# A replanned instruction order and moved query tiles in a one-core decoder trunk

## The chip, the cores and the metric

The kernel runs on one core of one Trainium2 chip. The time is the device time of one execution in microseconds (us). Five engines work side by side, each through its own instructions in program order: PE (matrix products, with PEld for its weight loads), DVE (vector work), ACT (activations and copies), POOL and SP, which here issues nearly all transfers.

## The reference

Two layers over x of 256 positions by 1024 channels. Each layer normalises x, multiplies it by one combined input matrix (1024 x 9808), runs three causal mixers of 8 heads with 64 channels each, gates each mixer's output, projects it to 1024 channels, merges the three by sigmoid gates, multiplies by an output matrix and adds the residual. A final normalisation follows.

```python
h = rms_norm(x, gain)
proj = jnp.einsum('bsd,de->bse', h, w_in)
(qa, ka, va, ga, qb, kb_, vb_, gb, qc, kc, vc, gc,
 q_idx, k_idx, w_idx, f_logit, merge_logit) = jnp.split(proj, SPLIT_POINTS, axis=-1)
oa = moba_attention(rope(qa), rope(ka), va) * jax.nn.silu(ga)              # with 256 positions: plain causal attention
ob = dsa_attention(rope(qb), rope(kb_), vb_, qi, ki, wi) * jax.nn.silu(gb) # the 64 best keys of each query by an index score
oc = forgetting_attention(qc, kc, vc, log_f) * jax.nn.silu(gc)             # a forget bias is added to the scores
y = jnp.einsum('nbsw,nwd->bsnd', jnp.stack([oa, ob, oc]), w_branch)
merged = jnp.sum(jax.nn.sigmoid(merge_logit) * y, axis=2)
return x + jnp.einsum('bsd,de->bse', merged, w_out)
```

## The kernel before

Everything is float32 in and out. To keep that precision PE multiplies split numbers: an operand is cut into a high part and a low remainder, and a product is high x high, low x high and high x low, three matmuls. The tiles ending in h and l (hTh and hTl, og0h and og0l, wh and wl) are such pairs.

Weights come from memory in pieces of 0.5 or 1 MB, read by SP into one of four raw tiles (line 436 for most). ACT writes the high part (wh, line 444) and DVE the remainder (wl, line 448); six tiles of each go round. PE multiplies from them at line 486 in units of 24 matmuls of 256 columns, or 12 for a branch projection, each unit into one of three proj tiles of PSUM. A proj tile comes free only when ACT or DVE has read the unit's result: line 986 (tanh of a merge gate into a mth tile, ACT), line 1017 (gate times branch projection, DVE), and others.

A mixer works on four pairs of heads. For a pair, `write_q` (line 683) makes three query tiles of 128 x 256: qh holds the high parts of both heads, and qx and qy are the tiles for the first and the second head, each with the high part of its head in one half of the partitions and a low part in the other. `scores` (line 698) runs six matmuls against the key tiles bd: the query tiles are the loaded weights, in two blocks of 128 columns, and the keys are streamed, 256 and 128 columns for the first block of queries and 512 and 256 for the second. Then come the softmax on DVE and ACT (lines 775 to 794, the last being the low part of the probabilities, "p lo"), one transfer that transposes each head's probabilities (line 803, issued by SP), the copies of the result into pt (lines 808 on ACT, 809 on DVE), and the eight matmuls of the product with the values, here called av (lines 821 to 824, two heads in turn). What follows av is the gating of the pair (lines 837 to 842, 476, 477).

The order of all instructions on every engine is fixed when the program is built. The kernel records some 3,300 operations with a key each; `Plan.run` places them one after the other by estimated costs and, among those of an engine that could start at about the same time, takes the smallest key. Two tables correct it: `SHIFT` adds a number to the key of the operation with that number, and `WAY` raises or lowers the cost of DVE for an operation that has DVE and another engine to choose from. The estimated costs themselves are not touched by the change. For wh and wl tiles a helper, `shifted`, states where the two sorts of tile begin:

```python
return [slice((a - base) % 512 // 4, (a - base) % 512 // 4 + 1024) for a, base in zip(at, (128, 0))]
```

wh tiles begin at 128 modulo 512 bytes of a partition, and wl tiles at 0. By the sizes of what stands between, all nine query tiles of before begin at 128.

Of the kernel before, what the change touches and what calls it, by code (L numbers as in the profile page):

```python
# [10 lines left out]
F32R = mybir.dt.float32r  # L11
# [5 lines left out]
S = 256  # L17
# [46 lines left out]
def constants(forget_bias):  # L64
# [24 lines left out]


SHIFT = {
# [31 lines left out]
}  # L123
WAY = {
# [6 lines left out]
}  # L131


# [173 lines left out]
def hybrid_trunk(ctx, tc, x, w_in, w_branch, w_out, final_gain, consts, out):  # L307
# [3 lines left out]
    pool = ctx.enter_context(tc.tile_pool(name="sb", bufs=1))  # L311
# [3 lines left out]
    plan = Plan()  # L315
# [32 lines left out]
    wh = [pool.tile([128, 1152], F32R, name=f"wh{i}") for i in range(R_RING)]  # L348
    fz = pool.tile([128, 6, 16], F32, name="fz")
    wl = [pool.tile([128, 1152], F32R, name=f"wl{i}") for i in range(R_RING)]  # L350
    ncs = pool.tile([128, 2, 8], F32, name="ncs")
    csum = pool.tile([128, 2, 8], F32, name="csum")
    V = [pool.tile([128, 2, 8, 128], F32R, name=f"v{i}") for i in range(2)]
    qs = [[pool.tile([128, S], F32R, name=f"q{p}{i}") for i in range(3)] for p in "hxy"]
    widx = pool.tile([128, 2, 8], F32, name="widx")
    hTh = pool.tile([128, KC, S], F32R, name="hTh")
    hTl = pool.tile([128, KC, S], F32R, name="hTl")
# [44 lines left out]
    tag("raw", R_RAW, [128, 2048])  # L402
    plan.tag("wh", wh)
    plan.tag("wl", wl)
    plan.tag("qx", qs[1])
    plan.tag("qy", qs[2])
    plan.tag("qh", qs[0])
    plan.tag("pt", pts)
    plan.tag("bd", bd)
    for nm, n, cols, dt in (("rsh", 2, S, F32), ("rr", 3, S, F32),  # L410
# [892 lines left out]
```

## Time and profile before

| | us |
|---|---|
| median of three runs | 602.27 |
| the three runs | 600.35, 602.92, 602.27 |
| the profiled execution | 601.2 |
| its span in the profile | 599.4 |
| PE busy | 587.5 |
| DVE busy | 542.3 |
| ACT busy | 463.8 |

The profile comes from one execution. A matmul's duration in it is longer than its turn on the engine, since matmuls overlap: what a matmul costs in a full row of them is the step from one start to the next. The wait table names, for each engine and line, what ended its idle time. The chain of waits goes back from the last instruction to what released it, step by step, and is a way to see which engine set the pace in each stretch. The granted clock of PE was full in every slice.

### The profile page before, as it was taken

How to read it: one execution, taken by the hardware profiler on the slowest of the kernel's cores; microseconds unless marked ns; L12 is line 12 of the kernel's file. 1: busy time of each engine (PE TensorE's matmuls, PEld its weight loads, DVE VectorE, ACT ScalarE, POOL GpSimd, SP SyncE). 2: the span in 40 equal slices, each digit the busy share in tenths (PEclk: the TensorE clock that was granted, in tenths of full speed). 3: DMA queues.
4: the chain of work that ended last, by engine and by line, in shares of the span. 5: the costliest groups of instructions: out<-in, count | busy, mean ns of one | idle time of the engine just before them, and what ended most of it. 6: DMA issues, size and time to landing. Idle time of an engine off the chain costs nothing.

```text
span 599.4 us, 12672 instructions
## 1 busy us (share of the span) xinstructions
PE 587.5 (98%) x4704; PEld 567.8 (95%) x4704; DVE 542.3 (90%) x1360; ACT 463.8 (77%) x1004; POOL 92.4 (15%) x102
## 2 busy tenths in 40 slices
PE   9999999999999999999999999999999999999995
PEld 7999999999998999999889999999999899999885
DVE  8889999989999989999686999999998999999773
ACT  5769669987997879985485874999889787999632
POOL 1042133000000225110000421320000023340000
PEclk9999999999999999999999999999999999999999
DMA  8986286597865866397648447669869486645802
GB/s 314 305 282 210 73 233 182 162 226 213 241 182 140 271 195 164 89 286 245 189 150 262 152 143 235 178 186 208 214 188 256 121 246 208 169 133 129 311 35 72
DMA packets 136510, 116.83 MB, mean 195 GB/s; under 512 B 42752, under 2 KB 127360, under 8 KB 136448
## 3 DMA queue, kind: packets, MB, share of 16 engines
q1 hardware_dynamic: 136160, 115.59, 66.4%
q8 instruction: 37, 0.61, 0.4%
q10 hardware_dynamic: 288, 0.43, 0.2%
q14 instruction: 25, 0.20, 0.1%
HBM read 103.42 MB, written 1.05 MB: 174 GB/s over the span
## 4 chain that ended last, share of the span: by engine, by line
PE 58%; DVE 22%; ACT 9%; DMA 5%; issue 4%; POOL 0%; SPq 0%; POOLq 0%; DVEq 0%; ACTq 0%
PE proj L486 47%; DVE wl L448 7%; PE proj L1173 4%; DMA t<-e 4%; ACT wh L444 2%; PE proj L1113 2%; DVE isc L970 2%; DVE e L794 1%; DVE rsh L535 1%; ACT pt L808 1%; ACT e L779 1%; DVE t L969 1%; DVE isc L949 1%; DMA raw<-in_w_out_dram 1%; DVE rr L537 1%
## 5 line engine op out<-in xcount | busy, mean ns | idle before, releaser
L486 PE MATMUL proj<-hTh,wh 128*128 128x256 f32 x1024 | 265.7, 278 | 1.5 <-ACT mth L986 1.0
L486 PE MATMUL proj<-hTl,wh 128*128 128x256 f32 x1024 | 265.0, 277 | 0.0
L448 DVE TENSOR_TENSOR wl<-raw,wh 128x1024 fp32r<-128x1024 f32 x180 | 223.3, 1249 | 15.2 <-ACT wh L444 14.0
L486 PE MATMUL proj<-hTh,wl 128*128 128x256 f32 x1024 | 227.9, 276 | 0.0
L444 ACT ACTIVATE wh<-raw 128x1024 fp32r<-128x1024 f32 x180 | 188.7, 1054 | 38.6 <-PE proj L486 26.3
L486 PEld LDWEIGHTS proj<-hTh,wh 128*128 128x128 f32 x1024 | 192.2, 188 | 2.3 <-ACT mth L986 1.2
L486 PEld LDWEIGHTS proj<-hTl,wh 128*128 128x128 f32 x1024 | 192.2, 188 | 0.0
L486 PEld LDWEIGHTS proj<-hTh,wl 128*128 128x128 f32 x1024 | 172.9, 188 | 0.0
L536 POOL TENSOR_TENSOR rsh<-rsh,cst 128x256 f32<-128x256 f32 x40 | 32.4, 812 | 351.4 <-DVE rsh L535 323.2
L538 POOL TENSOR_TENSOR rr<-rr,rsh 128x256 f32<-128x256 f32 x40 | 45.6, 1140 | 2.8
L779 ACT ACTIVATE e<-e,st 128x128 f32<-128x128 f32 (+1 forms) x96 | 42.6, 445 | 2.9 <-DVE st L775 2.4
L794 DVE SCALAR_TENSOR_TENSOR e<-e,st 128x128 f16<-128x128 f32 (+1 forms) x96 | 40.1, 424 | 1.1 <-ACT e L787 0.4
L808 ACT ACTIVATE pt<-t 128x384 fp32r<-128x384 f16 x73 | 34.3, 513 | 7.1 <-DMA t<-e 6.8
L486 PE MATMUL proj<-wh,v 128*128 128x512 f32 (+1 forms) x144 | 35.2, 366 | 0.0
L486 PE MATMUL proj<-og0l,wh 128*128 128x256 f32 x128 | 33.8, 277 | 0.0
L486 PE MATMUL proj<-og0h,wh 128*128 128x256 f32 x128 | 32.4, 278 | 1.3 <-DVE mth L1017 1.3
L787 ACT ACTIVATE e<-e,st 128x256 f16<-128x256 f32 (+1 forms) x77 | 31.6, 445 | 2.7 <-DVE st L783 2.3
L486 PEld LDWEIGHTS proj<-wh,v 128*128 128x128 f32 x144 | 25.3, 189 | 4.3
L486 PE MATMUL proj<-og0h,wl 128*128 128x256 f32 x128 | 28.6, 276 | 0.0
L486 PEld LDWEIGHTS proj<-og0h,wh 128*128 128x128 f32 x128 | 24.0, 188 | 1.6 <-DVE mth L1017 1.5
L486 PEld LDWEIGHTS proj<-og0l,wh 128*128 128x128 f32 x128 | 24.0, 188 | 0.0
L486 PEld LDWEIGHTS proj<-og0h,wl 128*128 128x128 f32 x128 | 21.7, 188 | 0.0
(227 smaller groups left out, 1071.0 us busy)
## 6 DMA issues: line engine op xcount, KB each, us to landing
raw<-in_w_in_dram SPq DMA_DIRECT2D x74, 1024.0 KB, 5.5
raw<-in_w_branch_dram SPq DMA_DIRECT2D x24, 512.0 KB, 4.2
raw<-in_w_out_dram SPq DMA_DIRECT2D x8, 1024.0 KB, 8.4
raw<-in_x_dram SPq DMA_DIRECT2D x8, 256.0 KB, 4.9
tmp<-wf SPq DMA_DIRECT2D x16, 128.0 KB, 5.5
t<-e SPq DMA_TRANSPOSE x48, 2.9
raw<-in_w_in_dram SPq DMA_DIRECT2D x2, 320.0 KB, 6.2
x<-in_x_dram SPq DMA_DIRECT2D x2, 256.0 KB, 3.8
```

The lines of the kernel that those rows point to most:

```text
L444: ACT.activation(p[0].v, sel(c.v), AF.Copy)
L448: DVE.tensor_tensor(p[1].v, sel(c.v), p[0].v.bitcast(F32), op=ALU.subtract)
L486: PE.matmul(o(), a(), b(), start=first and i == 0, stop=last and i == n - 1)
L536: gps(lambda: POOL.tensor_tensor(T(sh)[:np_], T(sh)[:np_], s[:np_], op=ALU.mult), S, [k_rope], [sh], key, "rope")
L538: gps(lambda: POOL.tensor_tensor(T(r)[:np_], T(r)[:np_], T(sh)[:np_], op=ALU.add), S, [sh], [r], key, "rope")
L779: act(lambda t=t, a=a, n=n, st=st, h=h: ACT.activation(ex(h, a, n), ex(h, a, n), AF.Exp, bias=T(st)[:, t:t + 1], scale=-1.0, accum_out=T(s ...
L787: ACT.activation(hi(a, n), ex(h, a, n), AF.Copy, scale=T(st)[:, 4 + t:5 + t])
L794: dve(lambda t=t, a=a, n=n, st=st, h=h, hi=hi, lo=lo: DVE.scalar_tensor_tensor(lo(a, n), ex(h, a, n), T(st)[:, 4 + t:5 + t], hi(a, n), op0 ...
L808: plan.op([("ACT", t_act(384, False), lambda to=to, src=src: ACT.activation(to(), src(), AF.Copy)), ("DVE", t_dve2(384), lambda to=to, src ...
L970: dve(lambda o=o, t8=t8: DVE.match_replace(o, T(t8), o, TAKEN), n, [t8], [k_isc[i]], key + r * step, "top8")
L1113: PE.matmul(T(ps[t]), h(i, t), v(w, n), start=left[t] == 23, stop=left[t] == 0)
L1173: PE.matmul(T(ps[t])[:, :w], hA[hi](a + x, t), T(p[wi])[:, ats[w > 256][wi]][:, :n * w].rearrange("p (k c) -> p k c", k=n)[:, x], start=le ...
```

## The change

Both tables are replaced, so that the order on each engine is another one while the operations, their estimated costs and the rules of the planner stay. The new numbers were found by replaying the program, outside the kernel, with a model that also counts the transfers by which the engines fetch their instructions. A few operations with a choice change their engine: in all, ACT has 73 rows of line 808 before and 72 after, DVE 23 and 24 of line 809, 28 and 27 of line 1019, 18 and 20 of line 842; POOL has 6 and 4 of line 841, 4 and 5 of line 1020.

Second, the six qx and qy tiles are allocated right behind the wl tiles, and so begin at 0 modulo 512 bytes. The three qh tiles stay behind the value tiles, at 128. All other tiles begin where they did modulo 512 bytes, and nothing else in the code changes. (The allocation gives some tiles another running number: v_78 becomes v_84.)

```diff
@@ -89,45 +89,44 @@
 SHIFT = {
-    0: -11.5, 1: -7, 3: -11.5, 4: -11, 17: 2, 28: -8, 31: -6, 47: -11, 73: 4, 80: -12, 89: -2.5, 90: -11.5, 91: 1.5,
...
+    0: -12, 1: -7.5, 3: -12, 4: -10.5, 18: -2.5, 19: -7.5, 22: -4.5, 28: -12, 31: -5.5, 38: -8, 46: -12, 47: -12,
...
 }
 WAY = {
-    17: -1500, 18: -1500, 90: -1500, 99: 1500, 489: 1500, 490: 1500, 539: 1500, 552: -1500, 553: -1500, 559: 1500,
...
+    18: 1500, 19: -1500, 46: 1500, 90: -1500, 126: -1500, 509: 1500, 534: -1500, 547: 1500, 548: -1500, 631: 1500,
...
 }
@@ -348,10 +347,11 @@
     wl = [pool.tile([128, 1152], F32R, name=f"wl{i}") for i in range(R_RING)]
+    qs = {p: [pool.tile([128, S], F32R, name=f"q{p}{i}") for i in range(3)] for p in "xy"}
     ncs = pool.tile([128, 2, 8], F32, name="ncs")
     csum = pool.tile([128, 2, 8], F32, name="csum")
     V = [pool.tile([128, 2, 8, 128], F32R, name=f"v{i}") for i in range(2)]
-    qs = [[pool.tile([128, S], F32R, name=f"q{p}{i}") for i in range(3)] for p in "hxy"]
+    qs.update({p: [pool.tile([128, S], F32R, name=f"q{p}{i}") for i in range(3)] for p in "h"})
@@ -402,9 +402,9 @@
-    plan.tag("qx", qs[1])
-    plan.tag("qy", qs[2])
-    plan.tag("qh", qs[0])
+    plan.tag("qx", qs["x"])
+    plan.tag("qy", qs["y"])
+    plan.tag("qh", qs["h"])
```

Three places of the order are spoken of below. The first is on ACT, in the first mixer of layer 0, around the first merge gate whose result goes to a mth tile (line 986). The other rows there are the copies of transposed probabilities (808), the key tiles of the third and fourth pair (852, 864), the second halves of query tiles (693, 695), the gating of the first pair (837, 476) and the high part of weights (444). Before:

```order
L808 ACTIVATE pt<-t_136 128x384 x2
L852 ACTIVATE bd1h<-rr_124 128x512
L693 ACTIVATE qx_84<-qy_87 64x256
L837 ACTIVATE ot_138<-o_159 64x256
L864 ACTIVATE bd1h<-bd1h 64x256
L693 ACTIVATE qx_83<-qy_86 64x256
L695 ACTIVATE qy_86<-qh_80 64x256
L864 ACTIVATE bd0h<-bd0h 64x256
L837 ACTIVATE ot_138<-o_159 64x256
L695 ACTIVATE qy_87<-qh_81 64x256
L864 ACTIVATE bd1h<-bd1h 64x256
L444 ACTIVATE wh_64<-raw_119 128x1024
```

and then og0h (line 476) and the two rows of line 986. After:

```order
L852 ACTIVATE bd0h<-rr_123 128x512
L864 ACTIVATE bd0h<-bd0h 64x256 x2
L808 ACTIVATE pt<-t_136 128x384
L986 ACTIVATE mth_143<-proj_152 128x256
L808 ACTIVATE pt<-t_137 128x384 x2
L444 ACTIVATE wh_68<-raw_119 128x1024
L695 ACTIVATE qy_80<-qh_87 64x256
```

The first merge gate, mth_143, has moved ahead of the second key tile, of the gating of the first pair and of one high part of weights. The second gate, mth_144, stands further back, behind the exponentials of the third pair.

The second place is on SP, at the transposes (803) of the third and fourth pair of the same mixer and the weight loads (436) between them. Before:

```order
L803 DMA_TRANSPOSE t_136<-e_128 128x6x128
L803 DMA_TRANSPOSE t_137<-e_128 128x6x128
L436 DMA raw_119<-in_w_in_dram 128x8x256
L803 DMA_TRANSPOSE t_136<-e_129 128x6x128
L436 DMA raw_117<-in_w_in_dram 128x8x256
L803 DMA_TRANSPOSE t_137<-e_129 128x6x128
```

After:

```order
L803 DMA_TRANSPOSE t_136<-e_128 128x6x128
L803 DMA_TRANSPOSE t_137<-e_128 128x6x128
L436 DMA raw_119<-in_w_in_dram 128x8x256
L803 DMA_TRANSPOSE t_136<-e_129 128x6x128
L803 DMA_TRANSPOSE t_137<-e_129 128x6x128
L436 DMA raw_117<-in_w_in_dram 128x8x256
```

The 1 MB load into raw_117 has moved from between the two transposes of the fourth pair to behind them. The second pair has the same kind of move: two loads stood between its transposes, and none does now.

The third place is on DVE, near the end of layer 1, where the remainders of the output matrix's pieces (wl, 448) meet the merge of the last branch (1017, 1019) and the gating of the last pair (839, 842, 477). Before:

```order
L842 TENSOR_TENSOR ot_139<-ot_139,g_127 128x256
L448 TENSOR_TENSOR wl_75<-raw_116,wh_68 128x1024
L477 SCALAR_TENSOR_TENSOR og0l<-ot_139,og0h 128x256
L448 TENSOR_TENSOR wl_71<-raw_118,wh_65 128x1024
L1017 SCALAR_TENSOR_TENSOR mth_143<-mth_143,proj_154 128x256
L1017 SCALAR_TENSOR_TENSOR mth_144<-mth_144,proj_153 128x256
L1019 TENSOR_TENSOR acc<-acc,mth_143 128x256
```

After:

```order
L842 TENSOR_TENSOR ot_139<-ot_139,g_127 128x256
L448 TENSOR_TENSOR wl_73<-raw_116,wh_67 128x1024
L477 SCALAR_TENSOR_TENSOR og0l<-ot_139,og0h 128x256
L1017 SCALAR_TENSOR_TENSOR mth_143<-mth_143,proj_152 128x256
L448 TENSOR_TENSOR wl_70<-raw_118,wh_63 128x1024
L1017 SCALAR_TENSOR_TENSOR mth_144<-mth_144,proj_153 128x256
L1019 TENSOR_TENSOR acc<-acc,mth_143 128x256
```

The product for mth_143 now stands ahead of the remainder of the piece in raw_118, the first of the output matrix, and the product for mth_144 still behind it. On PE, counted in matmuls of line 486 that stand ahead, the av groups of the four pairs of layer 0's first mixer stood at 534, 630, 732 and 774, and now stand at 570, 606, 720 and 756.

69 rows, old and new, of tables (SHIFT, WAY) are left out of this document.

## The prediction

> **What bounds the kernel now.** I read the page first: the span, the busy shares, the granted clock and the chain of waits.
>
> ```profile
> span 599.4 us, 12672 instructions
> PE 587.5 (98%) x4704; PEld 567.8 (95%) x4704; DVE 542.3 (90%) x1360; ACT 463.8 (77%) x1004; POOL 92.4 (15%) x102
> PE 58%; DVE 22%; ACT 9%; DMA 5%; issue 4%; POOL 0%; SPq 0%; POOLq 0%; DVEq 0%; ACTq 0%
> ```
>
> PE is the bound: it is busy for nearly all of the span, and the change gives it neither a matmul more nor one less. How tightly does it run? The chain has long stretches of nothing but PE, and one of them gives the step of a 256-column matmul; its last entries show what no order can touch.
>
> ```profile
> 44.01 5.45 PE proj L486 x48
> 587.34 6.78 issue
> ```
>
> 5.45 / 48 = 0.1135 us a matmul. What a new order can win is only the time in which PE stands still. The table of waits gives it for the weight loads, which come ahead of each matmul; the next-largest rows are mixed with the start of the program.
>
> ```profile
> PEld o L821 <- ACT pt L808: 1.7, 3, 0.7
> PEld proj L486 <- DVE mth L1017: 1.5, 1, 1.5
> PEld proj L486 <- ACT mth L986: 1.2, 1, 1.2
> PEld proj L486 <- DVE g L736: 1.0, 2, 0.6
> PEld proj L486 <- DVE rr L537: 0.5, 1, 0.5
> ```
>
> Each row is engine, line, who ended the wait, the sum in us, how many, the longest. Together 5.9 us, 1% of the span: that is about the ceiling of the order's part of the change, and it sits in few places. So I looked at each place in the timeline of PE.
>
> ```profile
> 101.02 0.39 PE L821 MATMUL o<-pt,v 128*128 128x256 f32 x1 [0.44 <-ACT pt L808]
> 111.20 0.38 PE L486 MATMUL proj<-hTh,wh 128*128 128x256 f32 x1 [1.02 <-ACT mth L986]
> 111.42 0.28 PE L486 MATMUL proj<-hTl,wh 128*128 128x256 f32 x1
> 134.30 0.38 PE L821 MATMUL o<-pt,v 128*128 128x256 f32 x1 [0.47 <-ACT pt L808]
> 563.87 0.39 PE L486 MATMUL proj<-og0h,wh 128*128 128x256 f32 x1 [1.34 <-DVE mth L1017]
> ```
>
> The bracket counts idle time from the modelled end of the matmul before, 0.28 after its start, where 0.11 would do; and the matmul behind a wait starts 0.22 later instead of 0.11 (111.20 to 111.42). A wait therefore costs its bracket plus 0.17 plus 0.11, the bracket plus 0.28: 0.72 at 101, 1.30 at 111, 0.75 at 134, 1.62 at 564. These four make 4.4 us, and what each hangs on is in the chain of waits.
>
> ```profile
> 93.39 4.31 DMA t<-e
> 104.02 0.94 ACT pt L808 x2
> 110.76 0.66 ACT mth L986 x2
> 127.87 5.77 DMA t<-e
> 133.73 0.53 ACT pt L808
> 553.30 7.85 DMA raw<-in_w_out_dram
> 561.17 1.07 ACT wh L444
> 562.26 1.23 DVE wl L448
> 563.49 0.34 DVE mth L1017
> ```
>
> At 101 and 134 PE stands before the product with the values, whose probabilities come late out of a transpose. At 111 it has no free proj tile, since ACT does other things before it reads a gate. At 564 it is the same with DVE, which is held by a weight remainder whose load landed late.
>
> **The change part by part: the order.** First pair of the first mixer (101): its av now has 36 more matmuls ahead of it, 36 x 0.1135 = 4.1 us of PE work against a lateness of 0.72. Its transposes are the ones at 93.39, and no load has been put between them. I take the whole 0.72. What comes late next could be the second pair, whose av moves 24 matmuls or 2.7 us forward; but two 1 MB loads that SP issued between its transposes are now behind them.
>
> The first gate (111): in the new order of ACT the gate stands directly behind one copy of probabilities, where before everything from 104.02 + 0.94 to 110.76 stood between, 5.8 us. PE has 12 matmuls of another unit, 1.4 us, between the unit that fills this proj tile and the next unit that needs it, so even a gate that is some tenths late costs nothing. The second gate has moved back, but PE has 24 + 12 matmuls of other units, 4.1 us, between its unit's two halves and the next use of its tile. I take 1.30.
>
> Fourth pair (134): the second transpose was issued behind a 1 MB load.
>
> ```profile
> 126.30 0.58 SPq L436 DMA_DIRECT2D raw<-in_w_in_dram  x1
> 127.87 1.22 SPq L803 DMA_TRANSPOSE t<-e  x1
> t<-e SPq DMA_TRANSPOSE x48, 2.9
> raw<-in_w_in_dram SPq DMA_DIRECT2D x74, 1024.0 KB, 5.5
> ```
>
> It took 5.77 to land where the median of all 48 is 2.9. With the load behind it, 2.9 us are won. PE arrives 18 matmuls earlier, 2.0 us, and was late by 0.75: 2.8 needed against 2.9 won, and DVE has two weight remainders less (2 x 1.2) ahead of the pair's last p lo. I take 0.75. The load itself starts later by about one transpose issue (1.22), and its weights are needed three raw tiles further on, which covers that.
>
> The last merge (564): the product for mth_143 no longer stands behind the remainder that ran at 562.26. It can free its proj tile as soon as its unit is done, and PE gets one unit of 12 matmuls, 1.36 us, before it needs the next tile. That product still stands behind the remainder, so it ends near 563.49 + 0.34, when PE has come to 562.37 + 1.36 = 563.73; with the slow restart some 0.3 is left. I take 1.3 of 1.62.
>
> Sum of the four: 0.72 + 1.30 + 0.75 + 1.3 = 4.1 us. Against it stands what the new order makes late elsewhere. There are 24 av groups, and the plan has little reserve before them. This is the last copy of probabilities and the av of the first pair of layer 0's second mixer:
>
> ```profile
> 167.28 0.35 DVE L809 CAST pt<-t 128x384 fp32r<-128x384 f16 x1
> 168.62 0.28 PE L821 MATMUL o<-pt,v 128*128 128x256 f32 x1
> ```
>
> 168.62 - 167.63 = 1.0 us to spare. The profile of before cannot show which of the 24 will now be missed. Between nothing and a return of all 4.1, I take one new wait of the size of the largest remaining kind, 0.7 at a pt copy plus its 0.28: 1.0 us, since the rows moved at the joints I compared in layer 1 stand within about a microsecond of work of where they stood. The dozen operations that change between ACT, DVE and POOL are half a microsecond each or so, on engines with 57 us (DVE, 599.4 - 542.3) and more of idle time; they cost nothing on PE while the four places above hold.
>
> The instruction fetches that the replay counts are real but small.
>
> ```profile
> q8 instruction: 37, 0.61, 0.4%
> q14 instruction: 25, 0.20, 0.1%
> ```
>
> That is 62 packets and half a percent of the engines' time, and the change moves no instruction out of the program, so they stay.
>
> **The query tiles.** What could the start of qx and qy change? They are weights of the score matmuls, and outputs and inputs of ACT and DVE.
>
> ```profile
> L486 PEld LDWEIGHTS proj<-hTh,wh 128*128 128x128 f32 x1024 | 192.2, 188 | 2.3 <-ACT mth L986 1.2 <-DVE rr L537 0.5 <-DVE g L736 0.4
> L486 PEld LDWEIGHTS proj<-hTh,wl 128*128 128x128 f32 x1024 | 172.9, 188 | 0.0
> L709 PEld LDWEIGHTS s<-bd0h,qx x24: 187/189/192, 49.3 to 536.3; 128*128 128x128 f32 x24
> L486 PE MATMUL proj<-wh,hTh 128*128 128x512 f32 x48 | 18.9, 395 | 0.2 <-DVE g L736 0.2
> L707 PE MATMUL s<-bd0l,qh 128*128 128x512 f32 x12 | 5.4, 453 | 0.1
> ```
>
> wh begins at 128 and wl at 0 modulo 512 bytes, and their loads take the same 188 ns, the query tiles' 189. But the 512-column score matmul takes 453 ns where the projection's takes 395, and during it the second block of qx is loaded. If that load's address is what costs 58 ns, the change can win 58 x 32 score groups = 1.9 us, and if the new address does the same to the 256-column ones it can lose as much. I take the row that is nearest, 188 against 188, and so nothing; both ends go into the range.
>
> The Trainium skill speaks against this part: "TensorE: Matmul & The Clock Gate", in its section on what happens when a matmul is issued, says that weight loads have a read port of their own and take nothing from the running matmul. By that the address is worth nothing either way. The 58 ns above are not explained by it.
>
> **Sum.** 4.1 - 1.0 = 3.1 us, 601.2 - 3.1 = 598.1 for an execution like the profiled one. The three runs and the profiled one average (600.35 + 602.92 + 602.27 + 601.2) / 4 = 601.7, and the profiled one lies 0.5 below that, so I predict **598.6 us**.
>
> **The rivals.**
>
> *The waits move.* Each av stands where the plan thinks the probabilities will just be there. If the copies come late at other pairs, the saved 4.1 come back as 0.7 to 1.0 at four or five of the 24. One place speaks for it: in layer 0's second mixer SP now has three loads, not one, between the first pair's two transposes. A load waits for its raw tile, by SP's own table
>
> ```profile
> SPq L436 <- DVE wl L448: 194.4, 48, 14.2
> ```
>
> 194.4 / 48 = 4.0 us a time. Two more loads are 8.1 us, and av there stands 30 matmuls or 3.4 us later and had 1 us to spare: 8.1 - 3.4 - 1 = 3.7 late. That alone gives 598.6 + 3.7 = 602.3, no change. Against it: the wait is for a tile that a PE unit ahead must release, and may be over by then. The Trainium skill, "Runtime: NRT & Kernel Launch", section on instruction fetch mechanics, says that the fetch is mostly hidden; then a plan that counts it has nothing to correct, which would also end here.
>
> *The score matmuls gain too.* The 58 ns go: 598.6 - 1.9 = 596.7. For it speaks 453 against 395, against it 188 against 188.
>
> *Slower.* The moved tiles take part in 128 of the 192 score matmuls. If a load from 0 modulo 512 cannot hide behind a matmul that streams the key tiles, each of the 128 costs 58 ns, 7.4 us: 598.6 + 7.4 = 606.0. It makes the kernel slower than before from 29 ns a load on (3.7 / 128), and by over 3 us from 52 ns on. Against it: wl tiles, at 0 as well, are loaded behind 256-column matmuls at the full rate.
>
> **How the numbers follow.** Forecast 0.46, waits move 0.28, score matmuls too 0.16, slower 0.10. I call faster or slower what differs by over 0.5%, about 3 us, which is what a measurement of this kernel can tell; that is below 599.3 or above 605.3. The forecast's own range is 597.6 to 600.6, the new waits being 0 to 3 us; about two thirds of it, 0.31, lies below 599.3. Faster: 0.31 + 0.16 + 0.01 of the second case = 0.48. Slower: 0.10 + 0.01. The rest, 0.41, is the same. For 8 in 10 the range goes from 595.4 (both gains and no new wait, 595.7, with a little for the spread of the runs) to 603.0 (waits moved, and the 0.65 by which the highest run lies above the median).
>
> **What would show it.** In the profile of the changed kernel: no wait over 0.5 of PE for line 986 near 111 and for line 1017 near 564, and the fourth pair's second transpose landing in about 3 us; waits of PE for pt of under 1.5 in all; the 512-column score matmul at 449 to 453 if the tiles do nothing, near 395 if they do. I am wrong if waits of PE sum to over 5 us again, if the first pair of layer 0's second mixer makes PE wait, or if the step between score matmuls changes by more than 20 ns.

## The result, and the profile after

The changed kernel takes **597.9 us** (median of six runs, 596.89 to 599.23) against 602.18 for the kernel before beside it: a ratio of 0.9935, 95% interval 0.9911 to 0.9958, 3.9 us less. Timed once more on another chip it was 0.9944 (0.9929 to 0.9959). The prediction was 598.6. The total was right; most of what it was added up from was not, and the sections below say where.

The page of the changed kernel: span, busy times, the shares of the chain of waits, and the median landing time of the transposes.

```profile
span 595.7 us, 12662 instructions
PE 585.9 (98%) x4704; PEld 567.3 (95%) x4704; DVE 539.4 (91%) x1362; ACT 464.6 (78%) x1003; POOL 92.3 (15%) x101
...
PE 82%; ACT 7%; DVE 6%; DMA 3%; issue 1%; POOL 1%; SPq 0%; POOLq 0%; DVEq 0%; ACTq 0%
...
t<-e SPq DMA_TRANSPOSE x48, 3.4
```

In this profile PE makes up 82% of the chain instead of 58%, and DVE 6% instead of 22%. In a second profile of each kernel, spoken of further below, PE's share is 70% before and 73% after. So the share changes more from one execution to the next than these two differ, and nothing is concluded from it here. PE has as many matmuls as before; it stands still less. The table of waits of the weight loads, in the columns explained above:

```profile
PEld proj L486 <- DVE mth L1017: 1.4, 1, 1.4
...
PEld o L821 <- DVE ot L839: 1.0, 1, 1.0
...
PEld proj L486 <- DVE acc L1012: 0.3, 2, 0.2
```

No row for pt and none for line 986 is left in this profile. The row for line 1017 reads like the one of before (1.5, once), but it is another wait: it stands at 239 us in layer 0, not at 564. The other row stands at 131 us, where the fourth pair of layer 0's first mixer still waits. The chain of waits shows what both hang on. First 131, then 239:

```profile
124.59 5.70 DMA t<-e
...
130.31 0.36 DVE pt L809
...
130.70 0.43 DVE ot L839
...
131.18 0.39 PE o L821
```

```profile
229.73 5.46 DMA t<-e
...
235.71 0.51 ACT pt L808
...
236.23 0.39 ACT ot L837
...
237.52 0.39 ACT ot L837
...
237.93 0.42 DVE ot L839
...
238.38 0.43 DVE mth L1017
...
238.85 1.21 PE proj L486 x8
```

At both places a transpose takes over 5 us (5.70 and 5.46), an engine that runs in program order waits for it at a copy of probabilities, and behind that copy stand the reads of the o tile (837, 839), of which there is only one in PSUM. At 131 PE waits for the o tile itself; at 239 DVE waits for ACT's second read, the merge (1017) stands behind DVE, and PE waits for the proj tile that the merge frees.

### The profile page after: what moved, and what is told of

It is laid out like the page before. It is cut to its first block, busy times and chain, and to the rows that moved or that the text cites. A ratio compares the mean times of both kernels' runs of the same rounds, so it can differ in the third digit from the quotient of the medians.

```text
span 595.7 us, 12662 instructions
## 1 busy us (share of the span) xinstructions
PE 585.9 (98%) x4704; PEld 567.3 (95%) x4704; DVE 539.4 (91%) x1362; ACT 464.6 (78%) x1003; POOL 92.3 (15%) x101
## 4 chain that ended last, share of the span: by engine, by line
PE 82%; ACT 7%; DVE 6%; DMA 3%; issue 1%; POOL 1%; SPq 0%; POOLq 0%; DVEq 0%; ACTq 0%
PE proj L486 69%; PE proj L1173 4%; PE proj L1113 2%; DMA t<-e 2%; ACT wh L444 2%; PE s L709 2%; PE s L707 2%; DVE wl L448 1%; PE o L821 1%; PE o L824 1%; ACT pt L808 1%; ACT e L779 1%; DVE isc L970 1%; DMA x<-in_x_dram 1%; ACT e L787 1%
## 5 line engine op out<-in xcount | busy, mean ns | idle before, releaser
L536 POOL TENSOR_TENSOR rsh<-rsh,cst 128x256 f32<-128x256 f32 x40 | 36.4, 910 | 300.5 <-DVE rsh L535 288.2
L538 POOL TENSOR_TENSOR rr<-rr,rsh 128x256 f32<-128x256 f32 x40 | 43.5, 1089 | 3.6 <-ACT qx L693 0.8
L787 ACT ACTIVATE e<-e,st 128x128 f16<-128x128 f32 (+1 forms) x76 | 31.0, 445 | 1.7 <-DVE e L794 0.7
L837 ACT ACTIVATE ot<-o 64x256 f32<-64x256 f32 x48 | 18.2, 380 | 6.4 <-PE o L824 4.3
```

Source lines behind the costliest of these rows:

```text
L536: gps(lambda: POOL.tensor_tensor(T(sh)[:np_], T(sh)[:np_], s[:np_], op=ALU.mult), S, [k_rope], [sh], key, "rope")
L538: gps(lambda: POOL.tensor_tensor(T(r)[:np_], T(r)[:np_], T(sh)[:np_], op=ALU.add), S, [sh], [r], key, "rope")
L787: ACT.activation(hi(a, n), ex(h, a, n), AF.Copy, scale=T(st)[:, 4 + t:5 + t])
L837: act(lambda r=r, h=h: ACT.activation(T(t)[r], T(o)[64:, h * S:(h + 1) * S], AF.Copy), S, True, [o], [kt[h]], key, "og", touch=[t], half=True)
```

## The experiments

Each ratio below is to the kernel before on the same chip, with its 95% interval; the kernel before took 600.6 to 602.2 us there. In no kernel is any work left out.

### The kernel before, once more

> The kernel before, unaltered, profiled a second time and timed against itself. Expected: a ratio of 1 with an interval that includes it, which shows what five rounds can tell. In the profile the waits at 101 and 111 us stand again, as in three other profiles of the old order of layer 0 (0.47 to 1.20 and 1.19 to 1.31 us). The one at 564 us stood at 1.50, under 0.1 and 0.59 us in three profiles of the old order of layer 1: if it belongs to the order it stands near 1.5 again, if to how one execution's loads landed it is under 1.0. The one at 134 us was 0.64 in the first profile of this kernel and 1.37 to 1.54 in the three others: here 0.6 if the first was typical of this program, 1.4 if not.

Ratio 0.9989 (0.9976 to 1.0002). So a comparison of this size tells some 0.15% or 0.9 us, and smaller effects are read from the traces alone. In its table of waits line 986 and pt stand again, and there is no row over 0.2 for line 1017. At the fourth pair the wait is 1.08, between the two values that were thought of:

```profile
PEld o L821 <- ACT pt L808: 2.0, 3, 1.1
PEld proj L486 <- ACT mth L986: 1.6, 1, 1.6
```

The next table gives the time between the starts of two matmuls beyond its usual value, in us, at the places that the argument rests on, for the profiles of both orders.

```
layer 0, first mixer and 239      101     111     131-136   239
before                            0.61    1.19    0.64      0.46
before, second profile            0.48    1.54    1.08      0.46
old order, new tiles              0.47    1.31    1.40      0.49
old layer 0, new layer 1          1.20    1.21    1.37      0.49
changed kernel                    none    none    0.97      1.33
changed kernel, second profile    none    none    0.98      1.31
new order, old tiles              none    none    0.96      1.41
new layer 0, old layer 1          none    none    0.93      1.58

layer 1, at 564, old order: before 1.50; second profile 0.06; with new tiles 0.09; with new layer 0: 0.59 (for og0l at 560)
```

The slow start behind a wait (0.11 at 111 us) is not in these numbers; it is in the terms of the prediction.

The waits at 101 and 111 belong to the order, and so do the new ones at 131 and 239. The one at 564 does not: the profile that the prediction read had it at 1.50, three other profiles at 0.6 or next to nothing.

### The order alone and the tiles alone

```diff
 order alone: both new tables, and
-    qs = {p: [pool.tile([128, S], F32R, name=f"q{p}{i}") for i in range(3)] for p in "xy"}
+    qs = [[pool.tile([128, S], F32R, name=f"q{p}{i}") for i in range(3)] for p in "hxy"]   # behind V, as before
 tiles alone: the old tables, and the new allocation
```

> Both new tables with the query tiles where they were before. In the trace of the changed kernel PE stands still 3.1 us less than before (8.5 against 11.6 us, summed over the stalls of PE), and the steps of running matmuls are 0.7 us shorter in all. Theory: the order carries the 3.1 and the tiles the 0.7, so this run is 3.1 us below the kernel before (about 599.0), and its 512-column score matmul steps at 287 ns again. Rival 1, the tiles carry the gain: within 1 us of before (601 to 602). Rival 2, the order is worth all of the 4.3 us between the medians: 597.9.

Ratio 0.9949 (0.9932 to 0.9966), 3.1 us less. The 512-column score matmul steps at 287 ns again, as expected.

> The old tables with the query tiles at their new start. Theory: only the running steps change, 4 ns on each 512-column score matmul, 5 ns on what follows it and 2 to 4 ns on some others, 0.7 us in all: about 601.4, which five rounds may not tell from no change. The waits of PE near 101, 111, 134 and 564 us stay. Rival 1: it gains 3 us or more (598 to 599). Rival 3, the tiles as such cost something that the new order hides: slower than before by 1 us or more.

Ratio 0.9998 (0.9987 to 1.0008): no change within 0.8 us. The order carries the gain. By the steps of the matmuls the tiles are worth little: the six matmuls of a score group and the step behind them take 914 ns instead of 927 in the first group, and 919 instead of 930 as the median of all 32: 11 ns x 32 = 0.35 us, which the timing cannot tell.

### One layer at a time

```diff
 SHIFT = {  # and WAY alike: entries below 1640 (layer 0) from the one table, the rest from the other
```

> The new tables for the operations of layer 0 and the old ones for layer 1, with the new query tiles. By the stalls of PE in the two traces layer 0 gains almost nothing, 6.1 against 6.0 us, since the waits at 101 and 111 us are replaced by new ones at 131 and 239 us; layer 1 goes from 5.5 to 2.6. Theory by these stalls: this run is 0.2 + 0.7 (tiles) = 0.9 us below before, 601.2. Rival, the prediction's own terms hold (2.8 us of its 4.1 lie in layer 0 and only the new wait of 1.3 against it): 2.8 - 1.3 + 0.7 = 2.2 below, 599.9.

Ratio 0.9973 (0.9960 to 0.9986), 1.6 us less: between the 0.9 of the theory and the 2.2 of its rival, and the interval (0.8 to 2.4) holds both.

> The converse: old tables for layer 0, new ones for layer 1, new query tiles. Theory by the stalls: 2.9 + 0.7 = 3.6 us below before, 598.5, and about as fast as the whole change. Rival by the prediction's terms: in layer 1 only the wait at 564 us was named, 1.3 + 0.7 = 2.0 below, 600.1. Rival 2, the new order of layer 1 works only behind that of layer 0: no gain, 601 to 602.

Ratio 0.9954 (0.9939 to 0.9969), 2.8 us less, again between theory (3.6) and rival (2.0), with both in the interval (1.9 to 3.7). So both layers gain. By the medians layer 1 gains more, where the prediction had named a single wait, but the two intervals overlap. Summing PE's time beyond the full rate over stretches (counted in us of PE work, four profiles of each order, the two runs above counted in each layer with the order that it has there) shows where:

```
stretch            0-80  80-160  160-240  240-320  320-520  520-560   sum
old order, mean    8.6   4.9     1.9      1.9      5.9      1.1       24.2
   lowest-highest  8.4-8.8  4.2-5.5  1.8-1.9  1.7-2.1  5.5-6.3  0.4-1.9
new order, mean    8.9   2.4     3.7      1.7      4.1      0.5       21.3
   lowest-highest  8.6-9.2  2.3-2.5  2.9-4.7  1.6-1.8  4.0-4.3  0.1-0.7
```

The first mixer of layer 0 (80 to 160) gives 2.5. The stretch with the wait at 239 takes 1.8 back, 0.9 of it at that wait, and the start 0.3. Layer 1 up to the last merge gives 1.8, in waits of 0.3 to 0.6 us and many of a tenth, none of which the prediction priced. The last merge gives 0.6 on average. The sum, 2.9, agrees with the 3.1 timed for the order alone.

### Two of the four moves, in the old order

The old order was written out row for row and two of the moves made by hand: on ACT both merge gates of 111 us (702, 709) go behind the second read of the first pair's o tile, and on DVE the last weight remainder (3160) behind the product for mth_143 (3102).

```diff
+MOVES = [("ACT", 702, 505), ("ACT", 709, 702), ("DVE", 3160, 3102)]   # the first goes right behind the second
```

> The kernel before with its order kept row for row except in two places: on ACT the two merge gates that PE waits for at 111 us stand right behind the second read of the first pair's o tile (4 rows and 2.3 us further forward), and on DVE the product for mth_143 near 564 us stands ahead of the weight remainder. By the prediction's terms (1.30 and 1.3) the two are worth 2.6 us: 598.7 where before is at 601.3. Theory from the traces so far: the wait at 111 goes, but part of it returns at the fourth pair's av (134 us), whose probabilities do not come earlier by as much; and the wait at 564 stood in one of three profiles of the old order of layer 1 (1.50, under 0.1 and 0.59 us), so it is worth about 0.7 and not 1.5: in all 1.0 to 1.5 us, 600. Rival: neither move counts, since what PE waits for next is set by the transfers: within 0.5 us of before.

Ratio 1.0014 (1.0002 to 1.0026): no gain at all, 0.9 us more if anything. In the profile the waits at 111 and 564 are gone, as meant. But at the fourth pair stands this (timeline of PE, and the chain behind it; line numbers are 163 higher here, 971 is the copy that was 808):

```profile
135.18 0.38 PE L984 MATMUL o<-pt,v 128*128 128x256 f32 x1 [1.37 <-ACT pt L971]
```

```profile
128.74 5.78 DMA t<-e
...
134.60 0.53 ACT pt L971
```

The wait there is 1.54, the highest with this order; in the two profiles of the kernel before it was 0.64 and 1.08. The transpose is issued 27.0 us after the av matmul at 101, as in the two profiles of before (26.9 and 27.3), and lands no faster; so PE arrives earlier and waits longer. Part of what the first move wins is given back there, 24 us later. How much is not settled: two more profiles of this order (see the table) have 1.40 and 1.37 at this place with the wait at 111 still standing, and the profiled execution, 599.84 us, was the fastest of the twelve, whose median is 601.47. What is shown is that the wait at 111, 1.2 to 1.5 us in every profile of the old order, can go without any gain in the median.

### The load behind the transposes, and the merge first

```diff
+HOLD = {821: 691}    # load behind: this operation isn't taken before that one (planner picks the rest anew)
+HOLD = {1239: 1442}  # merge first
```

> The changed kernel with one load more moved: the 1 MB load that SP issues at 121.85 us, ahead of the two transposes of the fourth pair (122.47 and 124.59 us, landing in 5.47 and 5.70), goes behind them. Theory, a transpose lands about 0.7 us after the load that was in flight when it was issued: with no load in flight both land in 2.7 to 3.0 us, up to 1.5 more with an instruction fetch between; the wait of PE at 131 us (0.97) is gone and the time is 0.5 to 1 us below the changed kernel's. Rival, the transposes are slow for another reason (the fetches alone, 0.01 and 5.3 us behind the first and 3.19 behind the second): they take over 4.5 us again and the wait stays. Second rival: the load, 4 us later, makes its weights late and PE waits for these instead, the same time or more.

Ratio 0.9948 (0.9931 to 0.9965), the same as the changed kernel's 0.9944 beside it. The first of these transposes landed in 2.76 and the second, with a fetch of instructions between, in 4.43, against 5.47 and 5.70. So the transposes were slow because of the load, the second one in part. But the wait grew to 1.52. Its chain (lines here are 3 higher than in the changed kernel):

```profile
124.31 4.43 DMA t<-e
...
128.76 0.36 DVE pt L812
129.12 1.13 DVE wl L451
...
130.28 0.43 DVE ot L842
...
130.76 0.38 PE o L824
```

The probabilities are there 1.5 us earlier, but the planner, which chose anew, has put a weight remainder between their copy and the second read of the o tile. It has also put this av group six matmuls (0.68 us) further forward, so PE comes earlier: the av matmul starts at 130.76 instead of 131.18 although the wait is longer. Neither theory nor rival foresaw that. The run shows what slowed the transposes; what the load's place is worth with all other rows kept, it does not show.

> The changed kernel with one operation of DVE moved: the merge (gate times branch projection, into mth) that PE waits for at 239 us stands ahead of the second addition of the pair's gating, for which DVE waits at 237.9. Theory, DVE is held by the operation ahead and PE by the proj tile: the merge runs about 1.3 us earlier, the wait of 1.33 falls under 0.3, and the time is 1.0 us below the changed kernel's. Rival, the unit that fills this tile ends late itself: the wait stays over 0.8 and the time too. Second rival, the gating's late part delays the next av through the single o tile and PE waits there.

Ratio 0.9941 (0.9925 to 0.9956), the same again. The wait of the proj tile is gone, and a wait for the o tile stands in its place (timelines of DVE and PE, lines 3 higher):

```profile
237.45 0.41 DVE L1020 SCALAR_TENSOR_TENSOR mth<-mth,proj 128x256 f32<-128x256 f32 x1
237.89 0.42 DVE L842 TENSOR_TENSOR ot<-o,ot 64x256 f32<-64x256 f32 x1
```

```profile
238.36 0.38 PE L824 MATMUL o<-pt,v 128*128 128x256 f32 x1 [0.85 <-DVE ot L842]
```

The merge runs 0.9 us earlier, and at the same microsecond PE waits for the o tile, as in the second rival. But the planner chose anew here too and put this av group 24 matmuls (2.7 us) further forward than in the changed kernel, where it starts at 241.72 without a wait. So the run does not tell whether the merge by itself would have won its 1.0 us.

### Both reads of the o tile ahead of the copies

```diff
+MOVES = [("SP", 821, 691), ("ACT", 721, 719), ("ACT", 822, 724), ("DVE", 722, 733),   # 131 us
+         ("ACT", 1270, 1238), ("ACT", 1271, 1270), ("DVE", 1442, 1400)]               # 239 us
```

> The changed kernel with its order kept row for row except for seven operations at the two waits that are left. At 131 us: the 1 MB load behind the transposes (as in the run that moved the load alone, with its high part later on ACT), and the second read of the third pair's o tile, on ACT and DVE, ahead of weight and probability copies. At 239 us: both reads of the o tile on ACT ahead of the next pair's two probability copies, which wait for a transpose, and the merge on DVE ahead of the second addition. Theory, both waits are one thing twice: the only o tile is read behind copies that wait for a late transpose, so that moving one operation alone only moves the wait; with both sides moved the stalls of 0.97 and 1.33 us go, 2.0 to 2.3 us below the changed kernel, about 596. Rival: PE then waits for the next thing at the same places (probabilities, proj tiles), and the gain is under 0.7 us.

In the profile both waits are gone (no stall over 0.2 at either place), which bears out that they were one thing twice. In time it won nothing: ratio 0.9960 (0.9944 to 0.9976). A new wait of 1.01 stands at 140 us. Its place on PE, a row of ACT's timeline, and the chain between (167 lines further down):

```profile
139.95 0.38 PE L653 MATMUL proj<-og0h,wh 128*128 128x256 f32 x1 [0.84 <-DVE g L903]
```

```profile
131.72 2.01 ACT L611 ACTIVATE wh<-raw 128x1024 fp32r<-128x1024 f32 x2 [1.24 <-DMA raw<-in_w_in_dram]
```

```profile
133.76 0.39 ACT ot L1004
...
138.43 1.14 DVE wl L615
139.57 0.33 DVE g L903
```

ACT now waits 1.24 for the load that was moved back, and everything on ACT and DVE behind its high part is later. That explains one of the two microseconds. Why none of the rest shows in the median (the profiled run itself was 596.68, the fastest of its six) stays open.

### What the 58 ns of the score matmul are

```diff
-            for o, sl, n in ((T(s0)[:, :256], slice(0, 128), 128), (T(s1), slice(128, 256), 256)):
+            for o, sl, n in ((T(s1), slice(128, 256), 256), (T(s0)[:, :256], slice(0, 128), 128)):
```

> The changed kernel with the two blocks of queries of a score group in the other order: the 512-column and two 256-column matmuls first, then the 256-column and the two 128-column ones. The sum of the work is the same. Theory: a weight load needs about 110 ns (from the load of the second block's qh, 335 ns into a group, to that of its qx at 446), a 128-column matmul streams for 57, so each of the two 128-column matmuls leaves some 55 ns of a weight load uncovered, and the profile books them on the matmuls behind; then the 512-column matmul, now behind a 256-column one, steps 227 to 232 ns instead of 283, the matmul that follows the last 128-column one takes the 55 ns instead, and the group as a whole stays at 914 ns within 15, with no change of time beyond 0.5 us. Rival: the 512-column matmul is slow in itself (its addresses or its columns): it keeps 283 ns wherever it stands.

The 512-column matmul in the changed kernel, and then the two places in this one (timelines of PE):

```profile
49.91 0.45 PE L707 MATMUL s<-bd0l,qh 128*128 128x512 f32 x1
50.20 0.28 PE L709 MATMUL s<-bd0h,qx 128*128 128x256 f32 x1
```

```profile
49.48 0.39 PE L707 MATMUL s<-bd0l,qh 128*128 128x512 f32 x1
49.70 0.28 PE L709 MATMUL s<-bd0h,qx 128*128 128x256 f32 x1
...
50.23 0.33 PE L486 MATMUL proj<-hTh,wl 128*128 128x256 f32 x1
50.40 0.28 PE L486 MATMUL proj<-hTh,wh 128*128 128x256 f32 x1
```

The step falls from 283 to 226 ns, and the projection matmul behind the last 128-column one takes 171 instead of 113. The group stays at 923 ns against 914; the ratio, 0.9958 (0.9944 to 0.9972), is near the changed kernel's. (These are the first group's; the medians are 924 and 919.) So the 58 ns are no matter of address and not of the 512 columns: they are the uncovered part of a weight load of about 110 ns behind a matmul that streams for 57. The Trainium skill, "TensorE: Matmul & The Clock Gate", section on loading the stationary operand, gives columns / 1.2 ns for a weight load, an estimate of 107 ns for 128 columns; the trace agrees, with 108 to 111 ns from the start of one load to the next around the 128-column matmuls. The prediction had taken from that page only that the load has a port of its own.

> The changed kernel's order with all nine query tiles at 192 modulo 512 bytes, where the key tiles begin that are streamed against them. With the query tiles at 128 the 512-column score matmul steps 287 ns, with qx and qy at 0 it steps 283, where 512 columns at the rate of the 256-column ones would take 227. Theory, what is loaded while a matmul streams costs nothing when both begin at the same place: the step falls to about 230 ns and 32 x 0.055 = 1.8 us are won. Rival, the start of a tile has to do with it only by the few ns seen so far: 283 to 288 ns and the same time within 0.5 us. Second rival, 192 is worse than both: over 290 ns, and slower.

282 ns, the rival: the step does not fall. The steps of the first block got longer (119, 61, 115 against 114, 57, 113). Ratio 0.9957 (0.9940 to 0.9973).

### The changed kernel, once more

> The changed kernel unaltered, timed beside the next three and profiled once more. Expected: 597 to 599 us, 3.9 below before; PE's waits at 131 us (0.97 us of stall in the first profile) and at 239 us (1.33) stand again, since they follow from the order; if they follow from how one execution's transfers happened to land, they change by more than half a microsecond.

As expected: 0.98 and 1.31, in the row "changed kernel, second profile" of the table above. One wait of 0.73 at 190 us stood in this profile and not in the first: a single execution holds waits of that size which another has not.

## Why the prediction was right, and where it was not

**What bounds the kernel, and the ceiling.** Right. PE has the same work and 3 us less idle time; nothing else became the bound.

**101 (0.72) and 111 (1.30).** The waits went, in every profile of the new order, and the one at 111 for the reason given. At 101 the reason was incomplete. ACT's rows of before show what PE waited for:

```profile
97.72 0.94 ACT L808 ACTIVATE pt<-t 128x384 fp32r<-128x384 f16 x2 [0.85 <-DMA t<-e]
98.57 1.99 ACT L444 ACTIVATE wh<-raw 128x1024 fp32r<-128x1024 f32 x2
100.47 0.92 ACT L808 ACTIVATE pt<-t 128x384 fp32r<-128x384 f16 x2
```

The second head's probabilities had landed at 98.57 (95.86 + 2.72), and their copy stood behind two high parts of weights. In the new order a load issued at 95.33 is in flight ahead of the pair's transposes, which land in 5.87 and 4.39 us instead of 4.31 and 2.72; the 36 matmuls more ahead of av cover that.

The worth of these waits was not shown to be their size: with the gates and the last merge moved in the old order, 111 was gone and nothing was won. The step that failed is to add waits of one stage as if each were paid by itself. In the stretch 80 to 160 the new order wins 2.5 us where the three terms there make 2.8, with a wait of 0.97 still standing at 131; it moves av groups, gates and transposes together, and which of them wins how much stays open.

**134 (0.75).** Wrong. "With the load behind it, 2.9 us are won": the load named did go behind the transposes, but another one, issued at 121.85, was in flight ahead of both, and they took 5.47 and 5.70. The step looked at the queue behind the transpose and not at what was still landing. And with the transposes made faster, PE stood for the o tile, in a run in which the planner had also changed other rows; only with both the load and the reads of the o tile moved was the wait at this place gone.

**564 (1.3).** The mechanism is right and the wait is gone. The size came from one execution: the stretch 520 to 560 has 0.4 to 1.9 us in the old order and 0.6 less on average in the new one.

**New waits (1.0).** Mis-sized. They come to some 2.1 us, 1.8 in the stretch up to 240 us and 0.3 at the start.

**What the sum left out.** Layer 1 between 320 and 520 us gives 1.8 us in waits of a few tenths. The table of waits of before had them in rows with no wait over 0.6, and in part in no row. So the sum had 0.3 (first mixer: 2.8 for 2.5), 0.7 (564: 1.3 for 0.6) and 1.1 (new waits: 1.0 for 2.1) too much, 2.1 us. It missed these 1.8 and 0.2 more between 240 and 320, 2.0 us. The total met by errors that cancel, and that is luck.

The instruction fetches were put at nothing because they take half a percent of the transfer engines' time. That reading was too short: a transpose that a fetch meets on its way lands up to 2.5 us later (last section), and the one at 93.39, from which the chain to the wait at 101 comes, was such a one.

**The query tiles.** Taken at nothing; timed at 0.1 us, with an interval from 0.8 less to 0.5 more. The rival "The score matmuls gain too", that the 58 ns go with the address, is refuted by the run with the blocks exchanged: they belong to a load behind a 128-column matmul, and go with every tile where it was. The rival "Slower", that a load from 0 costs as much, is refuted by the tiles alone, which cost no time.

**"The waits move".** It held elsewhere than was written. The place named, the first pair of layer 0's second mixer, did not wait. SP's queue there, and the last copy and the av group:

```profile
155.18 1.32 SPq L803 DMA_TRANSPOSE t<-e  x1
156.55 6.53 SPq L436 DMA_DIRECT2D raw<-in_w_in_dram  x3
163.14 3.91 SPq L803 DMA_TRANSPOSE t<-e  x2
```

```profile
170.70 0.62 DVE L809 CAST pt<-t 128x384 fp32r<-128x384 f16 x2
171.86 0.28 PE L821 MATMUL o<-pt,v 128*128 128x256 f32 x1
```

The two transposes are issued 8.0 us apart, where before they were 2.5 apart (157.24 and 159.78): two more loads cost 5.4 us and not 8.1. The first transpose goes out 2.1 us earlier, so the second is only 3.4 us later, which the 30 matmuls cover, and 171.86 - 171.32 = 0.5 us were to spare. Of the first mixer's gain of 2.5 us, 1.8 were instead given back in the stretch after it, half of that at 239.

**What would show it.** Of the tells, "no wait over 0.5 near 111 and 564" and "waits for pt under 1.5" held, the latter only by name: the wait for probabilities became one for the o tile behind a copy of probabilities. "Fourth pair's second transpose in about 3 us" failed (5.70). The 512-column score matmul went from 449 to 446. Of the three signs of being wrong none came: the rows of the wait table behind the start of the program, 5.9 us before, make 2.9 now (1.4, 1.0, 0.3 and 0.2), the first pair of the second mixer did not wait, and the score steps changed by 5 ns at most.

## What to carry to other kernels

A wait in a profile is worth its size only if nothing else is about as late at the same place or a little further on. Before adding up removed waits, move one by itself and look where the next wait of that stage stands. Keep all other rows as they are when you do: where the planner was left to choose anew, it moved av groups by six and by 24 matmuls, and the runs no longer priced the one move. And a wait in one profile is first to be found in a second profile of the same program: of four here, one was not there again.

## What the runs showed of the hardware

A transpose by the queue that also carries the loads lands behind the load that was in flight when it was issued: 4.70 us to the load's landing and 5.47 to the transpose's, and 4.64 and 6.79 where a fetch of instructions fell between the two landings. In the fourteen profiles 452 transposes were issued with a load in flight, and none landed less than 0.56 us behind it; 44 had no load, no other transpose and no fetch beside them and took 2.71 to 2.82 us. The median of all 48 of a profile rose from 2.9 to 3.4 although the order was made with the fetches counted. The Trainium skill, "DMA: Bandwidth & Descriptors", section on two DMAs through the same engine, says that descriptors of one queue start in order and are pipelined; that fits.

What a fetch of instructions does to a transpose depends on when it starts. Ten transposes were issued with no load or other transpose in flight and met one of the larger fetches (queue q8) that started 1.5 to 2.4 us behind their issue: they took 4.15 to 5.24 us. With the fetch starting earlier, at most 0.5 us behind the issue, 24 took 2.75 to 3.16. The Trainium skill, "Runtime: NRT & Kernel Launch", section on instruction fetch mechanics, has the fetch mostly hidden. The transfers that it meets are not spared here: in the profile of before, ACT waited 0.85 us at 97.72 for such a transpose, issued at 93.39 with a fetch at 95.38.
